# Half-Strassen first columns of the mixing product, and a new order of queue and products where attention ends and the branches begin

## The chip, the cores and the metric

The kernel runs on one core of a Trainium2 chip. The metric is the device time of one execution in microseconds (us). The five engines have one instruction stream each: PE (TensorE, matrix products), DVE (VectorE), ACT (ScalarE), POOL (GpSimd) and SP (SyncE, which here issues nearly all the DMA transfers). Each engine runs its own instructions in order, and they wait for each other through semaphores.

## The reference

The kernel computes one decoder block for 256 rows of width 2048 in float32. With the parts that the change leaves alone cut short:

```
proj = x @ w_in                         # 2048 columns each: bg, cg, hx, q, ..., ma, mb
y_a = (bg * causal_conv(cg * hx)) @ w_conv_out
y_b = sparse_attention(q, k, v, ...) @ w_attn_out
mixed = sigmoid(ma) * y_a + sigmoid(mb) * y_b
x = layer_norm(DN_ALPHA * x + mixed @ w_mix_out, ln1_g, ln1_b)
h = square(relu(x @ w_mlp_up)) @ w_mlp_down
ple = (p @ w_ple) * sigmoid(x @ w_ple_gate)
out = layer_norm(DN_ALPHA * x + h + ple, ln2_g, ln2_b)
```

## The kernel before

Every float32 operand of a matrix product is split into a high and a low part: ACT copies the high part, DVE subtracts it from the source to give the low part (`split`, L72 and L73). A product of two split operands takes three matmuls: high by high, low by high, high by low. The weights are read once from memory. `wchunk` (from L81) loads a chunk of 512 KB (`raw`, four buffers, DMA on SP, L85), copies it to `whi` (four buffers, ACT, L90) and subtracts to `wlo` (three buffers, DVE, L92). `xstat` takes 8 such chunks of 256 weight rows for 512 output columns: for each 128 weight rows it runs four matmuls with `whi` (L148, L149) and two with `wlo` (L152), and after the last chunk it evacuates two PSUM banks (one for each half of the 256 rows). `wstat` is the other layout (L110 with `whi`, L116 with `wlo`).

After attention come branch A (gate `ma`, weight `w_conv_out`, input `aT`) and branch B (gate `mb`, weight `w_attn_out`, input `oT`). In each branch, columns 0 to 1023 go as four blocks one after another: gate block 0 (L148 to L152 on `xT`, then a sigmoid on ACT, L707, into `sg`), out block 0 (L148 to L152 on `aT`, then a multiplication by `sg` on DVE, L776, into `ya`), gate block 1, out block 1. All four use PSUM banks 0 and 1, so the first matmul of a block waits for the evacuation of the block ahead of it. The gate's other 1024 columns are computed beside these blocks by Strassen's scheme (class `Seven`, L637 to L689, driven by `side()`): for each pair p of 128-row slices, a 1 MB load `rs` (L649, SP), sums of the input (`m` L714, `sa` L631 to L634), sums of the weights (`t`, L658 to L660), the splits of all of them into `forms` (L72, L73), and 18 matmuls (`products`, L676), where plain form takes 24. At the end `second` (L685) adds the seventh product, for which half of the weights are read again, and `close` combines the parts.

The two streams are interleaved by generators (`weave`, `next(sevens)`), but the order of the instructions on each engine is finally set by the compiler's scheduler, which simulates the kernel with its own costs; `after(ins)` tells it that an instruction may only come behind `ins` in that order.

After both branches the mixed rows (`mix`) are multiplied by `w_mix_out` in four plain `xstat` blocks of 512 columns (j = 0 to 3). Each is evacuated on DVE together with the residual `xres` (L861) and measured for the layer norm (L862).

Of the kernel before, what the change touches and what calls it, by code (L numbers as in the profile page):

```python
# [10 lines left out]
F32 = mybir.dt.float32  # L11
# [5 lines left out]
P = 128  # L17
# [28 lines left out]
def block_kernel(ctx: ExitStack, tc: tile.TileContext, x, p, w_in, conv_w, cmp_pe_k, cmp_w1_k, cmp_w2_k,  # L46
# [28 lines left out]

    last_hi, last_lo, last_whi, last_wlo, last_raw = [None], [None], [None], [None], [None]

# [3 lines left out]
    def wchunk(src, nk, n, behind=None):  # L81


        raw = wp.tile([P, nk, n], F32, tag="raw", name="raw", bufs=4)
        last_raw[0] = nc.sync.dma_start(raw, src).ins  # L85
        hi = wp.tile([P, nk, n], F32R, tag="whi", name="whi", bufs=4)
        lo = wp.tile([P, nk, n], F32R, tag="wlo", name="wlo", bufs=3)
        low, high = behind if isinstance(behind, tuple) else (behind, None)
        with after(high):
            last_whi[0] = nc.scalar.activation(hi, raw, AF.Copy).ins  # L90
        with after(low):
            last_wlo[0] = nc.vector.tensor_sub(lo, raw, f32(hi)).ins  # L92
        return hi, lo

    def wstat(src, c0, mov, evac, r0=0, nk=4, ahead=None, behind=None, ps=None):
# [6 lines left out]
        for k0 in range(0, KT, nk):  # L102
# [31 lines left out]

    def xstat(src, c0, n, sta, evac, r0=0, nkt=KT, ahead=None, behind=None, ps=None):

        if ps is None:
            ps = [mm([P, n]) for _ in range(NT)]
        for k2 in range(nkt // 2):
            hi, lo = wchunk(on_rows(src[r0 + k2 * 256:r0 + (k2 + 1) * 256, c0:c0 + n]), 2, n,  # L140
                            behind(k2) if behind is not None else None)
            for kk in range(2):
                kt = 2 * k2 + kk
                if ahead is not None:
                    ahead(kt)
                for t in range(NT):
                    ts = slice(t * P, (t + 1) * P)
                    nc.tensor.matmul(ps[t], sta[:, kt, 0, ts], hi[:, kk, :], start=(kt == 0), stop=False)  # L148
                    nc.tensor.matmul(ps[t], sta[:, kt, 1, ts], hi[:, kk, :], start=False, stop=False)  # L149
                for t in range(NT):  # L150
                    ts = slice(t * P, (t + 1) * P)
                    last_mm[0] = nc.tensor.matmul(ps[t], sta[:, kt, 0, ts], lo[:, kk, :], start=False,  # L152
                                                  stop=(kt == nkt - 1)).ins
            yield
        for t in range(NT):
            evac(t, ps[t])
# [44 lines left out]
    mhalf = const.tile([P, 1], F32, name="mhalf")  # L201
    nc.gpsimd.memset(mhalf, -0.5)

    X = big.tile([P, KT, 2, T], F32R, tag="X", name="xT")
# [268 lines left out]
    def attend(j, q):  # L473
# [111 lines left out]
        for g in range(4):  # L585
# [51 lines left out]
    class Seven:  # L637

        def __init__(self, rows, c0, mat, raw, t, forms, b, t0):
            self.rows, self.c0, self.mat, self.raw, self.t, self.forms, self.b, self.t0 = (
                rows, c0, mat, raw, t, forms, b, t0)
            self.raws, self.ts, self.sums, self.acc = {}, {}, {}, {}

        def load(self, p):
            self.raws[p] = self.raw(p)
            with after(last_raw[0]):
                nc.sync.dma_start(self.raws[p], self.rows[:, p, :, self.c0:self.c0 + 1024])  # L649

# [15 lines left out]
        def products(self, p, which):  # L666
            b, t0 = self.b(p), self.t0
            for n in which:
                first = (self.mat[:, 2 * p, :, 0:P] if n == 1 else self.mat[:, 2 * p + 1, :, P:] if n == 4 else
# [5 lines left out]
                for i, (a, w) in enumerate(((0, hi), (1, hi), (0, lo))):  # L675
                    last_mm[0] = nc.tensor.matmul(self.acc[n], first[:, a, :], self.forms[:, w, :],  # L676
                                                  start=(p == 0 and i == 0), stop=(p == 7 and i == 2)).ins

        def second(self, ps):

            for q in range(0, 8, 2):
                hi, lo = wchunk(self.rows[:, q:q + 2, 1, self.c0:self.c0 + 512], 2, 512)
                for k in range(2):
                    for i, (a, w) in enumerate(((0, hi), (1, hi), (0, lo))):
                        last_mm[0] = nc.tensor.matmul(ps, self.mat[:, 2 * (q + k) + 1, a, 0:P], w[:, k, :],  # L685
                                                      start=(q + k == 0 and i == 0),
                                                      stop=(q + k == 7 and i == 2)).ins
                yield
# [4 lines left out]
    def gate_seven(c_gate, raw):  # L693
        return Seven(in_pairs(w_in), c_gate + 1024, X, raw,
                     lambda p: [post.tile([P, 2, 512], F32, tag="m2", name="t") for _ in range(2)], None,
                     lambda p: 0, 4)

    def branch(c_gate, w, sta, sv, g, put, after_seven, last_two, close_at, meanwhile=lambda: iter(())):

        sg, forms = {}, sv.forms

        def gate_block(j):
            sg[j] = post.tile([P, NT, 512], F32, tag="sg", name="sg")
            return xstat(w_in, c_gate + j * 512, 512, X,
                         lambda t, ps: nc.scalar.activation(sg[j][:, t, :], ps, AF.Sigmoid), ps=[bank(0), bank(1)])  # L707
# [4 lines left out]
        def x_sums(p):  # L712
            m = post.tile([P, 2, T], F32, tag="pT", name="m", bufs=1)
            nc.vector.tensor_add(m, f32(X[:, 2 * p:2 * p + 2, 0, :]), f32(X[:, 2 * p:2 * p + 2, 1, :]))  # L714
            sv.sums[p] = forms[:, 12 + p % 2 * 2:14 + p % 2 * 2].rearrange("p a (c b t) -> p (a c) b t", c=2, b=2)
            sums_to(m, sv.sums[p])

        def side():

            if not sv.raws:  # L720
                sv.load(0)
                yield
            for i in range(4 * 8 + 1):
                p, r = divmod(i, 4)
                if r == 0 and p > 0:
                    sv.products(p - 1, (5, 7, 6, 4))
                if p < 8:
                    if r == 0:
                        x_sums(p)
                        sv.b_forms(p)  # L730
                    elif r == 1:
                        sv.t_sums(p)
                        if p < 7:
                            sv.load(p + 1)
                    elif r == 2:
                        sv.t_forms(p)
                    else:
                        sv.products(p, (1, 3))
                yield

        sevens = side()
# [99 lines left out]
    split(tp, pT[:, :, 0, :], pT[:, :, 1, :])  # L841
    C = post.tile([P, 2, NT * D], F32, tag="C", name="ple_gb", bufs=1)
    ple = C[:, 0].rearrange("p (t d) -> p t d", t=NT)
    gb = C[:, 1].rearrange("p (t d) -> p t d", t=2)
    y = post.tile([P, NT, D], F32, tag="Y", name="y", bufs=1)
# [10 lines left out]

    for j in range(4):
# [273 lines left out]
```

## Time and profile before

| | |
|---|---|
| Median of 3 runs | 1809.9 us (1809.32 to 1810.31) |
| Profiled execution, its own time | 1808.84 us |
| Span of its trace, first to last instruction | 1806.6 us |
| Busy share of PE, DVE, ACT | 99%, 74%, 55% |

The trace of one execution lies behind all the rows below. A matmul's own duration of 0.39 us is its latency through the array; a stream of matmuls of 512 columns starts one every 0.23 us, so it is the distance between starts that counts. In a timeline row, the text in square brackets is the idle time ahead of the instruction and what ended it. Rows named PEld, the weight loads, run beside the matmuls.

### The profile page before, as it was taken

The page shows a single profiled execution, that of the slowest core. Times are in us where ns is not written, and L with a number is a line of the kernel's source. Part 1 is how long each engine was busy: PE and PEld are TensorE (multiplying, and loading weights), DVE is VectorE, ACT ScalarE, POOL GpSimd, SP SyncE. Part 2 cuts the span into 40 slices and gives each one's busy share as a digit, 9 for nine tenths or more (in the row PEclk, how much of TensorE's full clock was granted, in tenths as well). Part 3 has the DMA queues.
Part 4 walks back from the last instruction along what each step waited for, and adds up shares of the span by engine and source line. Part 5 has one row for each costly group of instructions (what it writes and reads, how often), then busy time and mean ns, then how long its engine had stood idle before and what let it go on. Part 6 is the DMA issues. An engine that isn't in the chain of part 4 may idle for free.

```text
span 1806.6 us, 24945 instructions
## 1 busy us (share of the span) xinstructions
PE 1790.7 (99%) x9292; PEld 1534.9 (85%) x9292; DVE 1339.0 (74%) x1964; ACT 989.8 (55%) x1342; POOL 18.4 (1%) x33
## 2 busy tenths in 40 slices
PE   9999999999999999999999999999999999999997
PEld 7889888888888788888888888888888888888886
DVE  6776776767787996897755668886898689865564
ACT  5555555555555555555443745764676467646640
POOL 1000000000000000000000000000000000000000
PEclk9999999999999999999999999999999999999999
DMA  8777665566655665866655577754865586567671
GB/s 258 225 239 210 183 176 164 164 182 179 175 163 173 200 233 176 278 201 225 193 183 195 176 242 239 228 187 162 281 209 163 186 268 216 173 205 219 220 242 54
DMA packets 256121, 363.41 MB, mean 201 GB/s; under 512 B 10837, under 2 KB 175541, under 8 KB 255232
## 3 DMA queue, kind: packets, MB, share of 16 engines
q1 hardware_dynamic: 250944, 348.30, 61.5%
q0 software_dynamic: 2112, 8.81, 1.4%
q10 hardware_dynamic: 2944, 4.72, 0.8%
q8 instruction: 73, 1.20, 0.3%
q14 instruction: 48, 0.39, 0.1%
HBM read 359.66 MB, written 2.12 MB: 200 GB/s over the span
## 4 chain that ended last, share of the span: by engine, by line
PE 99%; DVE 0%; ACT 0%; DMA 0%; issue 0%; SPq 0%; DVEq 0%
PE mm L110 16%; PE u L110 9%; PE s L676 9%; PE mm L116 8%; PE u L148 7%; PE u L149 7%; PE u L152 7%; PE u L116 5%; PE s L152 5%; PE s L149 5%; PE s L148 5%; PE s L110 4%; PE s L116 2%; PE s L685 2%; PE s L1073 1%; PE pss L497 1%
## 5 line engine op out<-in xcount | busy, mean ns | idle before, releaser
L92 DVE TENSOR_TENSOR wlo<-raw,whi 128x1024 fp32r<-128x1024 f32 (+2 forms) x588 | 702.0, 1201 | 305.6 <-issue 69.0
L90 ACT ACTIVATE whi<-raw 128x1024 fp32r<-128x1024 f32 (+2 forms) x588 | 612.1, 1043 | 530.2 <-PE u L149 160.8
L110 PE MATMUL mm<-xT,whi 128*128 128x512 f32 x1280 | 313.2, 393 | 0.0
L110 PEld LDWEIGHTS mm<-xT,whi 128*128 128x128 f32 x1280 | 234.0, 189 | 44.7 <-ACT whi L90 0.6
L110 PE MATMUL u<-x,whi 128*128 128x512 f32 x736 | 190.7, 391 | 0.0
L116 PE MATMUL mm<-xT,wlo 128*128 128x256 f32 x1280 | 181.6, 285 | 0.6 <-DVE wlo L92 0.6
L116 PEld LDWEIGHTS mm<-xT,wlo 128*128 128x128 f32 x1280 | 169.8, 190 | 8.2 <-DVE wlo L92 0.8
L110 PEld LDWEIGHTS u<-x,whi 128*128 128x128 f32 x736 | 132.5, 188 | 23.2
L116 PEld LDWEIGHTS u<-x,wlo 128*128 128x128 f32 x736 | 101.8, 190 | 8.2
L116 PE MATMUL u<-x,wlo 128*128 128x256 f32 x736 | 104.2, 282 | 0.0
L73 DVE TENSOR_TENSOR forms<-tr,forms 128x1024 fp32r<-128x1024 f32 x68 | 81.7, 1221 | 16.1 <-ACT forms L72 15.8
L72 ACT ACTIVATE forms<-tr 128x1024 fp32r<-128x1024 f32 x68 | 70.4, 1050 | 18.3 <-PE s L676 8.6
L676 PE MATMUL s<-forms,sums 128*128 128x512 f32 x288 | 73.0, 390 | 0.0
L110 PE MATMUL s<-x,whi 128*128 128x512 f32 x288 | 71.6, 392 | 0.0
L676 PEld LDWEIGHTS s<-forms,sums 128*128 128x128 f32 x288 | 53.7, 188 | 11.1
L148 PE MATMUL s<-whi,h 128*128 128x512 f32 x160 | 62.2, 389 | 0.0
L149 PE MATMUL s<-whi,h 128*128 128x512 f32 x160 | 62.2, 389 | 0.0
L110 PEld LDWEIGHTS s<-x,whi 128*128 128x128 f32 x288 | 52.2, 188 | 9.7
L148 PE MATMUL u<-whi,xT 128*128 128x512 f32 x128 | 49.9, 390 | 0.6 <-DVE cg L463 0.6
L149 PE MATMUL u<-whi,h 128*128 128x512 f32 x128 | 49.8, 389 | 0.0
L149 PE MATMUL u<-whi,xT 128*128 128x512 f32 x128 | 49.8, 389 | 0.0
L676 PE MATMUL s<-forms 128*128 128x512 f32 x192 | 49.6, 389 | 0.0
(347 smaller groups left out, 2990.4 us busy)
## 6 DMA issues: line engine op xcount, KB each, us to landing
raw<-in_w_in_dram SPq DMA_DIRECT2D x204, 512.0 KB, 4.4
raw<-in_w_mlp_up_dram SPq DMA_DIRECT2D x128, 512.0 KB, 4.6
raw<-in_w_mlp_down_dram SPq DMA_DIRECT2D x84, 512.0 KB, 4.1
raw<-in_w_conv_out_dram SPq DMA_DIRECT2D x32, 512.0 KB, 4.3
raw<-in_w_attn_out_dram SPq DMA_DIRECT2D x32, 512.0 KB, 4.4
raw<-in_w_mix_out_dram SPq DMA_DIRECT2D x32, 512.0 KB, 3.7
raw<-in_w_ple_gate_dram SPq DMA_DIRECT2D x32, 512.0 KB, 4.4
rs<-in_w_mlp_down_dram SPq DMA_DIRECT2D x12, 1024.0 KB, 7.3
```

What stands on the lines that cost most here:

```text
L72: last_hi[0] = nc.scalar.activation(hi, src, AF.Copy).ins
L73: last_lo[0] = nc.vector.tensor_sub(lo, src, f32(hi)).ins
L90: last_whi[0] = nc.scalar.activation(hi, raw, AF.Copy).ins
L92: last_wlo[0] = nc.vector.tensor_sub(lo, raw, f32(hi)).ins
L110: last_mm[0] = nc.tensor.matmul(ps[f].rearrange("p a t -> p (a t)"), hi[:, kk, f * P:(f + 1) * P], mov[:, k0 + kk].rearrange("p a t -> p ( ...
L116: last_mm[0] = nc.tensor.matmul(ps[f][:, 1, :], lo[:, kk, f * P:(f + 1) * P], mov[:, k0 + kk, 0, :], start=False, stop=False, skip_group_c ...
L148: nc.tensor.matmul(ps[t], sta[:, kt, 0, ts], hi[:, kk, :], start=(kt == 0), stop=False)
L149: nc.tensor.matmul(ps[t], sta[:, kt, 1, ts], hi[:, kk, :], start=False, stop=False)
L152: last_mm[0] = nc.tensor.matmul(ps[t], sta[:, kt, 0, ts], lo[:, kk, :], start=False, stop=(kt == nkt - 1)).ins
L497: nc.tensor.matmul(ps, q[:, g, a, t * P:(t + 1) * P], kT[:, j, c, c0:c0 + n], start=(i == 0), stop=(i == 2))
L676: last_mm[0] = nc.tensor.matmul(self.acc[n], first[:, a, :], self.forms[:, w, :], start=(p == 0 and i == 0), stop=(p == 7 and i == 2)).ins
L685: last_mm[0] = nc.tensor.matmul(ps, self.mat[:, 2 * (q + k) + 1, a, 0:P], w[:, k, :], start=(q + k == 0 and i == 0), stop=(q + k == 7 and ...
```

## The change

- `Seven` takes a number of pairs n, and a new object `sv_mix` with n = 4 computes rows 0 to 1023 of columns 0 to 1023 of the mixing product by Strassen's scheme, beside the plain blocks for columns 1024 to 2047. Rows 1024 to 2047 of the first columns stay plain (`mix_block` with k0 = 8). `mix_close` combines the parts. Its 1 MB loads are named `tr`. `side` moves out of `branch`.
- The residual `xres` moves to another place in memory (tag C), behind `oT`.
- Where attention ends: the first gate chunk is issued by `prefetch` inside the last attention turn; the first `rs`, `m`, `sa`, `sg` and `t` get the first places of the new pool; a sigmoid of one column (`mhalf1`) stands ahead of the branches; and the fifth chunk of gate block 0 may be issued only behind the first `rs` load (`held`).
- `seven_a.lag = 1`: in branch A the products come one step later in the order, and each may only stand behind the last matmul that was written before it (`behind`).
- `wstat`: the last chunk of a projection with `ahead` (the first one only) takes the high part ahead of the low part.

```
         raw = wp.tile([P, nk, n], F32, tag="raw", name="raw", bufs=4)
-        last_raw[0] = nc.sync.dma_start(raw, src).ins
+        with after(held[0]):
+            last_raw[0] = nc.sync.dma_start(raw, src).ins
+        held[0] = None
...
             last = k0 + nk == KT
-            parts_ = (low, high) if last or ahead is None and k0 // nk % 2 == 1 else (high, low)
+            parts_ = (low, high) if last and ahead is None or ahead is None and k0 // nk % 2 == 1 else (high, low)
...
+    def prefetch():
+        first_piece.append(wchunk(on_rows(w_in[:256, C_MA:C_MA + 512]), 2, 512))
+        yield
+    first_piece = []
...
-            weave(chain(*dense), evenly(20, 4 * len(dense)), attend(j, q))
+            weave(chain(*dense), evenly(20, 4 * len(dense)) + [23] * (j == 3),
+                  chain(attend(j, q), prefetch()) if j == 3 else attend(j, q))
...
+    rs0 = post.tile([P, 2, 1024], F32, tag="rs", name="rs", bufs=1)
+    m0 = post.tile([P, 2, T], F32, tag="pT", name="m", bufs=1)
+    sa0 = post.tile([P, 4, P], F32, tag="pn", name="sa", bufs=1)
     ya = post.tile([P, NT, D], F32, tag="Y", name="ya", bufs=1)
+    sg0 = [post.tile([P, NT, 512], F32, tag="sg", name="sg") for _ in range(2)]
+    t0 = [post.tile([P, 2, 512], F32, tag="m2", name="t") for _ in range(2)]
+    with after(last_hi[0]):
+        nc.scalar.activation(mhalf1, mhalf, AF.Sigmoid)
...
         def products(self, p, which):
             b, t0 = self.b(p), self.t0
+            behind = last_mm[0] if self.lag else None
             for n in which:
                 first = (self.mat[:, 2 * p, :, 0:P] if n == 1 else self.mat[:, 2 * p + 1, :, P:] if n == 4 else
                          self.sums[p][:, {5: 0, 6: 1, 7: 2, 3: 3}[n]])
...
                 if p == 0:
                     self.acc[n] = bank({1: 2, 3: 3, 5: 4, 7: 5, 6: 6, 4: 7}[n])
                 for i, (a, w) in enumerate(((0, hi), (1, hi), (0, lo))):
-                    last_mm[0] = nc.tensor.matmul(self.acc[n], first[:, a, :], self.forms[:, w, :],
-                                                  start=(p == 0 and i == 0), stop=(p == 7 and i == 2)).ins
+                    with after(behind):
+                        last_mm[0] = nc.tensor.matmul(self.acc[n], first[:, a, :], self.forms[:, w, :],
+                                                      start=(p == 0 and i == 0), stop=(p == self.n - 1 and i == 2)).ins
...
+    def side(sv, tag):
...
+        for _ in range(sv.lag):
+            yield
+        for i in range(4 * sv.n + 1):
+            p, r = divmod(i, 4)
...
+        ahead_of = None
+        if not sv.raws:
+            sv.load(0)
+            ahead_of, first_load = 3, sv.last_load
+        sevens = side(sv, "pT")
         for j in range(2):
             for block in (lambda: gate_block(j), lambda: out_block(j, [bank(0), bank(1)])):
-                for _ in block():
+                for i, _ in enumerate(block()):
                     next(sevens)
+                    if i == ahead_of:
+                        held[0], ahead_of = first_load, None
...
-    seven_a = gate_seven(C_MA, lambda p: post.tile([P, 2, 1024], F32, tag="rs", name="rs", bufs=1))
+    seven_a = gate_seven(C_MA, lambda p: post.tile([P, 2, 1024], F32, tag="rs", name="rs", bufs=1) if p else rs0)
+    seven_a.lag = 1
...
-    xres = big.tile([P, NT, D], F32, tag="O", name="xres")
+    xres = post.tile([P, NT, D], F32, tag="C", name="xres", bufs=1)
...
+    sv_mix = Seven(in_pairs(w_mix_out), 0, mix, lambda p: tr[-1][:, p % 2],
+                   lambda p: [post.tile([P, 2, 512], F32, tag="m2", name="t") for _ in range(2)],
+                   big.tile([P, 16, 512], F32R, tag="X", name="forms"), lambda p: 0, 4, n=4)
+    def mix_block(j, banks, k0=0, ahead=None):
         cs = slice(j * 512, (j + 1) * 512)
-        def ev_mix(t, ps):
-            nc.vector.scalar_tensor_tensor(y[:, t, cs], xres[:, t, cs], ALPHA, ps, op0=ALU.mult, op1=ALU.add)
+        def ev(t, ps):
+            if k0:
+                nc.vector.tensor_add(y[:, t, cs], y[:, t, cs], ps)
+            else:
+                nc.vector.scalar_tensor_tensor(y[:, t, cs], xres[:, t, cs], ALPHA, ps, op0=ALU.mult, op1=ALU.add)
             nc.vector.bn_stats(stats[:, t, j, :], y[:, t, cs])
-        run(xstat(w_mix_out, j * 512, 512, mix, ev_mix, ahead=mix_turn({4: (3, sg[3], 0), 8: (3, sg[3], 2)}) if j == 0 else None))
+        return xstat(w_mix_out, j * 512, 512, mix, ev, r0=k0 * P, nkt=KT - k0, ps=banks, ahead=ahead, kt0=k0)
+    def mix_close():
+        a = sv_mix.acc
+        u = [post.tile([P, 2, 512], F32, tag="m2", name="u") for _ in range(2)]
+        u2, u3, u4 = u[0][:, 0], u[0][:, 1], u[1][:, 0]
+        at = [(t, slice(c, c + 512)) for t in range(2) for c in (0, 512)]
+        y00, y01, y10, y11 = (y[:, t, c] for t, c in at)
+        x00, x01, x10, x11 = (xres[:, t, c] for t, c in at)
+        nc.scalar.activation(u2, a[1], AF.Copy)
+        for dst, v, w, op in ((y00, x00, a[1], ALU.add), (u2, u2, a[6], ALU.add), (u4, u2, a[5], ALU.add),
+                              (y11, x11, a[5], ALU.add), (y01, x01, a[3], ALU.add), (u3, u2, a[7], ALU.add),
+                              (y10, x10, a[4], ALU.subtract), (y01, y01, u4, ALU.add), (y10, y10, u3, ALU.add),
+                              (y11, y11, u3, ALU.add)):
+            with after(last_wlo[0]):
+                if v in (x00, x01, x10, x11):
+                    nc.vector.scalar_tensor_tensor(dst, v, ALPHA, w, op0=ALU.mult, op1=op)
+                else:
+                    nc.vector.tensor_tensor(dst, v, w, op=op)
+        yield
+        ps = bank(4)
+        for i, _ in enumerate(sv_mix.second(ps)):
+            if i < 1:
+                yield
+        nc.vector.tensor_add(y00, y00, ps)
+        yield
+    sv_mix.load(0)
+    weave(chain(mix_block(2, [bank(0), bank(1)], ahead=mix_turn({4: (3, sg[3], 0), 8: (3, sg[3], 2)})),
+                mix_block(3, [bank(0), bank(1)]), mix_block(0, [bank(0), bank(1)], 8),
+                mix_block(1, [bank(2), bank(3)], 8)),
+          list(range(20)), chain(side(sv_mix, "sg"), mix_close()))
+    C = post.tile([P, 2, NT * D], F32, tag="C", name="ple_gb", bufs=1)
+    ple = C[:, 0].rearrange("p (t d) -> p t d", t=NT)
+    gb = C[:, 1].rearrange("p (t d) -> p t d", t=2)
```

How the instructions stand on the engines before and after is shown at two places. Names: `raw`, `whi` and `wlo` are a weight chunk and its parts, `rs` the load for the products, `m` and `sa` sums of the input, `t` sums of the weights, `forms` their split parts. Line numbers of the changed kernel differ: L86 is L85 of before, L94 is L92, L672 is L649, L681 to L683 are L658 to L660, L727 is L714, L654 to L657 are L631 to L634, L153, L154 and L157 are L148, L149 and L152, L701 is L676, L760 is L707.

First place: the end of attention and gate block 0. On SP, the queue of loads, before:

```order
L85 DMA raw<-in_w_in_dram 128x2x512 x8
L649 DMA rs<-in_w_in_dram 128x2x1024
L85 DMA raw<-in_w_conv_out_dram 128x2x512 x4
L649 DMA rs<-in_w_in_dram 128x2x1024
L85 DMA raw<-in_w_conv_out_dram 128x2x512 x3
```

The same place on SP now:

```order
L86 DMA raw<-in_w_in_dram 128x2x512 x4
L672 DMA rs<-in_w_in_dram 128x2x1024
L86 DMA raw<-in_w_in_dram 128x2x512 x4
L672 DMA rs<-in_w_in_dram 128x2x1024
L86 DMA raw<-in_w_conv_out_dram 128x2x512 x4
```

The first `rs` load has moved ahead of chunks 5 to 8 of gate block 0.

On DVE at the same place, from the first `m` of branch A, before (the first `wlo` here is that of chunk 5):

```order
L714 TENSOR_TENSOR m<-xT 128x512
L92 TENSOR_TENSOR wlo<-raw,whi 128x1024
L631 TENSOR_TENSOR sa<-m 128x128
L633 TENSOR_TENSOR sa<-m 128x128
L632 TENSOR_TENSOR sa<-sa,m 128x128
L634 TENSOR_TENSOR sa<-m,sa 128x128
L714 TENSOR_TENSOR m<-xT 128x512
L92 TENSOR_TENSOR wlo<-raw,whi 128x1024
L658 TENSOR_TENSOR t<-rs 128x1024
```

On DVE now, from the sixth instruction behind that first `m` on (the `wlo` at the end is that of chunk 5):

```order
L73 TENSOR_TENSOR forms<-sa,forms 128x4x128
L654 TENSOR_TENSOR sa<-m 128x128
L656 TENSOR_TENSOR sa<-m 128x128
L655 TENSOR_TENSOR sa<-sa,m 128x128
L681 TENSOR_TENSOR t<-rs 128x1024
L657 TENSOR_TENSOR sa<-m,sa 128x128
L73 TENSOR_TENSOR forms<-rs,forms 128x1024
L682 TENSOR_TENSOR t<-rs,t 128x512
L727 TENSOR_TENSOR m<-xT 128x512
L73 TENSOR_TENSOR forms<-t,forms 128x1024
L683 TENSOR_TENSOR t<-t,rs 128x512
L94 TENSOR_TENSOR wlo<-raw,whi 128x1024
```

The `wlo` of chunk 5, which stood ahead of the first instruction that needs `rs`, now stands behind seven instructions that begin with it.

Second place: the end of gate block 0 and the start of out block 0 in branch A. On PE, before (`u<-wlo,xT` is gate block 0, `u<-whi,aT` is out block 0, `s<-forms` are the products):

```order
L149 MATMUL u<-whi,xT 128x512
L152 MATMUL u<-wlo,xT 128x512 x2
L676 MATMUL s<-forms 128x512
L676 MATMUL s<-forms,xT 128x512 x3
L676 MATMUL s<-forms 128x512 x2
L676 MATMUL s<-forms,xT 128x512
L676 MATMUL s<-forms 128x512 x5
L148 MATMUL u<-whi,aT 128x512
```

On PE now:

```order
L153 MATMUL u<-whi,xT 128x512
L154 MATMUL u<-whi,xT 128x512
L153 MATMUL u<-whi,xT 128x512
L154 MATMUL u<-whi,xT 128x512
L157 MATMUL u<-wlo,xT 128x512 x2
L153 MATMUL u<-whi,aT 128x512
```

The twelve products that stood between the two blocks have moved into the blocks; nothing stands between the last matmul of the one and the first of the other.

On ACT at this place, now (`sg<-u` is the evacuation of gate block 0):

```order
L72 ACTIVATE forms<-t 128x1024
L72 ACTIVATE forms<-sa 128x4x128
L92 ACTIVATE whi<-raw 128x1024 x2
L760 ACTIVATE sg<-u 128x512 x2
L92 ACTIVATE whi<-raw 128x1024
```

Two chunk copies (L92) stand directly ahead of the two sigmoids; before, a split (`forms<-t`) and the table load of the sigmoid stood there.

## Rows read from the trace of the kernel before

**Rows 1.** The page: busy times, and engines of the chain that ended last.

```profile
PE 1790.7 (99%) x9292; PEld 1534.9 (85%) x9292; DVE 1339.0 (74%) x1964; ACT 989.8 (55%) x1342; POOL 18.4 (1%) x33
...
PE 99%; DVE 0%; ACT 0%; DMA 0%; issue 0%; SPq 0%; DVEq 0%
```

**Rows 2.** Waits of PE: us in total, times, longest us.

```profile
PE u L148 <- ACT sg L707: 0.7, 1, 0.7
PE mm L116 <- DVE wlo L92: 0.6, 1, 0.6
```

**Rows 3.** Windows: length, busy PE, PEld, DVE, ACT, POOL, granted clock, DMA share, GB/s.

```profile
625.00:650.00 25.00, 25.00 (x112) 20.70 (x111) 25.00 (x34) 14.67 (x16) 0.00 (x0) 1.00 0.64 213
915.00:940.00 25.00, 25.00 (x118) 20.69 (x117) 14.55 (x17) 10.68 (x12) 0.00 (x0) 1.00 0.54 177
940.00:1005.00 65.00, 65.00 (x289) 53.81 (x288) 36.01 (x37) 25.25 (x25) 0.00 (x0) 1.00 0.59 193
```

**Rows 4.** Timeline of the mixing product: start us, duration us, engine, line, instruction.

```profile
999.76 0.39 PE L148 MATMUL s<-whi,mix 128*128 128x512 f32 x1
...
1001.12 0.39 PE L148 MATMUL s<-whi,mix 128*128 128x512 f32 x1
```

**Rows 5.** Timeline of the first projection's last chunk.

```profile
21.53 0.68 DVE L92 TENSOR_TENSOR wlo<-raw,whi 128x512 fp32r<-128x512 f32 x1
22.27 0.74 PE L116 MATMUL mm<-xT,wlo 128*128 128x256 f32 x4 [0.63 <-DVE wlo L92]
22.84 0.40 PE L110 MATMUL mm<-xT,whi 128*128 128x512 f32 x1
```

**Rows 6.** Timeline of the end of attention and gate block 0.

```profile
578.28 0.87 PE L576 MATMUL po<-pT,vn 128*128 128x256 f32 x6
...
579.22 0.37 SPq L649 DMA_DIRECT2D rs<-in_w_in_dram  x1
...
584.45 1.22 DVE L658 TENSOR_TENSOR t<-rs 128x1024 f32<-128x1024 f32 x1 [0.64 <-DMA rs<-in_w_in_dram]
...
585.59 0.68 DVE L73 TENSOR_TENSOR forms<-sa,forms 128x512 fp32r<-128x512 f32 x1
585.80 0.62 PE L152 MATMUL u<-wlo,xT 128*128 128x512 f32 x2
...
586.19 1.22 DVE L73 TENSOR_TENSOR forms<-rs,forms 128x1024 fp32r<-128x1024 f32 x1
```

**Rows 7.** Timeline of the end of gate block 0 and the start of out block 0.

```profile
599.62 0.39 PE L676 MATMUL s<-forms,xT 128*128 128x512 f32 x1
600.04 1.04 ACT L90 ACTIVATE whi<-raw 128x1024 fp32r<-128x1024 f32 x1
...
600.99 1.04 ACT L72 ACTIVATE forms<-t 128x1024 fp32r<-128x1024 f32 x1
...
602.05 1.28 ACT L707 ACT_TABLE_LOAD   x1
...
603.34 1.09 ACT L707 ACTIVATE sg<-u 128x512 f32<-128x512 f32 x2
...
603.99 0.50 PE L148 MATMUL u<-whi,aT 128*128 128x512 f32 x1 [0.70 <-ACT sg L707]
```

**Rows 8.** DVE's instructions by line and form, 570 to 915 us: busy us, mean ns, idle before.

```profile
L92 DVE TENSOR_TENSOR wlo<-raw,whi 128x1024 fp32r<-128x1024 f32 x104 | 126.8, 1221 | 40.3 <-PE u L152 21.3 <-PE s L152 10.2 <-issue 4.6
...
L714 DVE TENSOR_TENSOR m<-xT 128x512 f32<-128x512 f32 x16 | 11.0, 684 | 3.4 <-PE po L576 3.4
...
L631 DVE TENSOR_TENSOR sa<-m 128x128 f32<-128x128 f32 x16 | 4.5, 284 | 0.0
...
L776 DVE TENSOR_TENSOR ya<-u,sg 128x512 f32<-128x512 f32 x4 | 2.6, 685 | 1.3 <-PE u L152 1.3
```

**Rows 9.** PE's timeline at the start of the kernel.

```profile
6.84 2.05 PE L110 MATMUL mm<-xT,whi 128*128 128x512 f32 x4
8.68 1.06 PE L116 MATMUL mm<-xT,wlo 128*128 128x256 f32 x4
```

More of the change, by code (lines that the diff above doesn't have):

```diff
@@ L74, in split @@
         return last_lo[0]
-    last_hi, last_lo, last_whi, last_wlo, last_raw = [None], [None], [None], [None], [None]
+    last_hi, last_lo, last_whi, last_wlo, last_raw, held = ([None] for _ in range(6))
     def on_rows(src):
@@ L133, in wstat, with xstat @@
             evac(f, ps[f][:, 0, :], ps[f][:, 1, :])
-    def xstat(src, c0, n, sta, evac, r0=0, nkt=KT, ahead=None, behind=None, ps=None):
+    def xstat(src, c0, n, sta, evac, r0=0, nkt=KT, ahead=None, behind=None, ps=None, kt0=0, first=None):
         if ps is None:
@@ L139, in xstat @@
         for k2 in range(nkt // 2):
-            hi, lo = wchunk(on_rows(src[r0 + k2 * 256:r0 + (k2 + 1) * 256, c0:c0 + n]), 2, n,
-                            behind(k2) if behind is not None else None)
+            if first is not None and k2 == 0:
+                hi, lo = first
+            else:
+                hi, lo = wchunk(on_rows(src[r0 + k2 * 256:r0 + (k2 + 1) * 256, c0:c0 + n]), 2, n,
+                                behind(k2) if behind is not None else None)
             for kk in range(2):
@@ L147, in xstat @@
                     ts = slice(t * P, (t + 1) * P)
-                    nc.tensor.matmul(ps[t], sta[:, kt, 0, ts], hi[:, kk, :], start=(kt == 0), stop=False)
-                    nc.tensor.matmul(ps[t], sta[:, kt, 1, ts], hi[:, kk, :], start=False, stop=False)
+                    nc.tensor.matmul(ps[t], sta[:, kt0 + kt, 0, ts], hi[:, kk, :], start=(kt == 0), stop=False)
+                    nc.tensor.matmul(ps[t], sta[:, kt0 + kt, 1, ts], hi[:, kk, :], start=False, stop=False)
                 for t in range(NT):
                     ts = slice(t * P, (t + 1) * P)
-                    last_mm[0] = nc.tensor.matmul(ps[t], sta[:, kt, 0, ts], lo[:, kk, :], start=False,
+                    last_mm[0] = nc.tensor.matmul(ps[t], sta[:, kt0 + kt, 0, ts], lo[:, kk, :], start=False,
                                                   stop=(kt == nkt - 1)).ins
@@ L202, in block_kernel @@
     nc.gpsimd.memset(mhalf, -0.5)
+    mhalf1 = const.tile([P, 1], F32, name="mhalf1")
     X = big.tile([P, KT, 2, T], F32R, tag="X", name="xT")
@@ L637, in block_kernel, with __init__ @@
     class Seven:
[L641 to L644, printed above, removed]
+        def __init__(self, rows, c0, mat, raw, t, forms, b, t0, n=8):
+            self.rows, self.c0, self.mat, self.raw, self.t, self.forms, self.b, self.t0, self.n = (
+                rows, c0, mat, raw, t, forms, b, t0, n)
+            self.raws, self.ts, self.sums, self.acc, self.lag = {}, {}, {}, {}, 0
         def load(self, p):
@@ L648, in load @@
             with after(last_raw[0]):
-                nc.sync.dma_start(self.raws[p], self.rows[:, p, :, self.c0:self.c0 + 1024])
+                self.last_load = nc.sync.dma_start(self.raws[p], self.rows[:, p, :, self.c0:self.c0 + 1024]).ins
         def b_forms(self, p):
@@ L686, in second @@
                                                       start=(q + k == 0 and i == 0),
-                                                      stop=(q + k == 7 and i == 2)).ins
+                                                      stop=(q + k == self.n - 1 and i == 2)).ins
                 yield
@@ L696, in gate_seven, with x_sums @@
                      lambda p: 0, 4)
+    def side(sv, tag):
+        def x_sums(p):
+            m = post.tile([P, 2, T], F32, tag=tag, name="m", bufs=1 if tag == "pT" else 2)
+            nc.vector.tensor_add(m, f32(sv.mat[:, 2 * p:2 * p + 2, 0, :]), f32(sv.mat[:, 2 * p:2 * p + 2, 1, :]))
+            sv.sums[p] = sv.forms[:, 12 + p % 2 * 2:14 + p % 2 * 2].rearrange("p a (c b t) -> p (a c) b t", c=2, b=2)
+            sums_to(m, sv.sums[p])
+        for _ in range(sv.lag):
+            yield
+        for i in range(4 * sv.n + 1):
+            p, r = divmod(i, 4)
+            if r == 0 and p > 0:
+                sv.products(p - 1, (5, 7, 6, 4))
+            if p < sv.n:
+                if r == 0:
+                    x_sums(p)
+                    sv.b_forms(p)
+                elif r == 1:
+                    sv.t_sums(p)
+                    if p < sv.n - 1:
+                        sv.load(p + 1)
+                elif r == 2:
+                    sv.t_forms(p)
+                else:
+                    sv.products(p, (1, 3))
+            yield
     def branch(c_gate, w, sta, sv, g, put, after_seven, last_two, close_at, meanwhile=lambda: iter(())):
-        sg, forms = {}, sv.forms
+        sg = {}
         def gate_block(j):
@@ L706, in gate_block @@
             return xstat(w_in, c_gate + j * 512, 512, X,
-                         lambda t, ps: nc.scalar.activation(sg[j][:, t, :], ps, AF.Sigmoid), ps=[bank(0), bank(1)])
+                         lambda t, ps: nc.scalar.activation(sg[j][:, t, :], ps, AF.Sigmoid), ps=[bank(0), bank(1)],
+                         first=first_piece.pop() if first_piece else None)
         def out_block(j, banks, ahead=None):
             return xstat(w, j * 512, 512, sta, lambda t, ps: put(j, t, ps, sg[j][:, t, :]), ps=banks, ahead=ahead)
[L712 to L741, printed above, removed]
+        ahead_of = None
[3 more added lines that the diff above has]
+        sevens = side(sv, "pT")
         for j in range(2):
             for block in (lambda: gate_block(j), lambda: out_block(j, [bank(0), bank(1)])):
-                for _ in block():
+                for i, _ in enumerate(block()):
                     next(sevens)
+                    if i == ahead_of:
+                        held[0], ahead_of = first_load, None
         run(sevens)
@@ new lines, in mix_close @@
+    def mix_close():
[13 more added lines that the diff above has]
+                    nc.vector.scalar_tensor_tensor(dst, v, ALPHA, w, op0=ALU.mult, op1=op)
+                else:
+                    nc.vector.tensor_tensor(dst, v, w, op=op)
[5 more added lines that the diff above has]
+        nc.vector.tensor_add(y00, y00, ps)
+        yield
```

7 lines of the change are left out of this document (2 added, 5 removed).

## The prediction

> **What bounds the kernel now.** I read the page first, then PE's waits, then timelines of the places that the change touches, and last windows for the density of DVE. The page says that PE is busy for 99% of the span and that the chain that ended last is 99% PE [rows 1]. So a microsecond is won only by fewer matmuls or by a wait of PE that goes, and lost by a wait of PE that comes. The waits are few and short: in the stretch that is changed, one of 0.7 us for a sigmoid and one of 0.6 us for a `wlo` [rows 2]. The price of a matmul is the distance of starts: from 999.76 to 1001.12 us six of them begin, L148 to L152 and two more, so 1.36 / 6 = 0.227 us [rows 4]. DVE, which prepares the products, has 50.6 of 90 us busy in the mixing product but 25.00 of 25 in a stretch of branch A, and PE still does not wait there [rows 3].
>
> **Mixing product.** Before: 4 blocks x 16 slices x 6 = 384 matmuls. Now: 192 for the last two column blocks, 96 for the plain half of the first two, 4 pairs x 18 = 72 products and 12 for the seventh, together 372. Twelve fewer at 0.227 are -2.7 us. On DVE each pair costs `m` 0.68, four `sa` at 0.28, the split of the sums 0.68, of the weights 1.22, `t` 1.22 + 0.68 + 0.68 and two splits at 1.22, together 8.7 us (128x1024 forms at 1.22, 128x512 at 0.68, 128x128 at 0.28) [rows 8]. Four pairs are 34.9, the close adds 11 operations at 0.68 or 7.5, and six `wlo` fewer (eight chunks go, two come for the seventh product) take off 7.3. The 50.6 us become 85.7, in about 87 us. That is close to full. As the branch ran at 25.00 of 25 without a wait [rows 3], and as the preparation of the first pairs stands in branch B's last block, I take 0. Bounds: 0, and for blocks 2 and 3 alone (half of the old 50.6 + 34.9 = 60.2, with the two turns of `mix` some 2.7 more, against 264 matmuls or 59.9) 3 us, 5 with the 2 that the last closing operations could add behind the last matmul. `xres` is loaded later, by ACT, 2 MB that are needed only at the first evacuation some 27 us (120 matmuls) on; I count nothing, and price a miss as part of the 5.
>
> **First projection.** PE waits to 22.27 for a `wlo` that DVE starts at 21.53 and ends at 22.21, and then does four low matmuls [rows 5]. With the four high ones first (4 x 0.227 = 0.9 us) this time is filled, and the wait of 0.6 us goes: -0.6 (bounds -0.8 and 0). Late next is the same `wlo`, which is then done ahead of its reader by 0.3 us.
>
> **The old waits around 600 us.** Between 599.62 and 603.99 us PE starts 11 matmuls, 2.49 us of work in 4.37 us, so 1.88 us go to waits, for `forms` and for the sigmoid behind a table load of 1.28 us [rows 7]. The table load moves ahead of the branch (the one-column sigmoid `mhalf1`), where ACT has time, and the products stand one step later, so their forms are there: -1.9 (bounds -1.9 and -1.2, with the `forms` waits kept).
>
> **Start of branch A: a new wait.** In the order of SP the first `rs` load stands ahead of chunks 5 to 8. It still waits for the last matmul of attention, L576: before, it was issued at 579.22, right behind that matmul's end at 579.15, and landed at 584.45 [rows 6]. Its new place in the pool does not free it, since the semaphore that its row in the order waits for still counts to that matmul. So `rs` does not come earlier, and what is queued behind it comes later. On DVE the `wlo` of chunk 5 stands behind the seven instructions that begin with `t<-rs`. In one stream such instructions start 1.14 us apart for 128x1024 (584.45 to 585.59) and 0.60 for 128x512 (585.59 to 586.19) [rows 6]; `sa` I take at 0.2. From the landing: 1.14 + 0.2 + 1.14 + 0.6 + 0.6 + 1.14 + 0.6 = 5.4, so the `wlo` begins at 589.9 and ends at 591.1. PE wants it at 585.80 [rows 6], and its order has nothing else there: 591.1 - 585.8 = +5.3 us. Behind the waiting L152 stand the rest of gate block 0 and the products; behind the `wlo` on DVE the next two, which PE then reaches later than they end. ACT is less late: the chunk's raw data, half as large, lands by estimate half of 5.2 us behind `rs`, the `whi` copy of 1.04 us is done near 588.2 [rows 6, 7], and four matmuls of chunk 5 fall into the wait. Bounds: 0, if the order on DVE costs nothing, and 6.9, an estimate, if `rs` takes 30% longer than its 5.2 us beside the loads that are now issued right behind it. [...]
>
> **Block ends in branch A: three new waits.** All blocks share banks 0 and 1. Before, products stood between the blocks and filled PE's time while ACT or DVE emptied the banks. Now they stand in closed groups inside the blocks, and PE goes straight from the last L152 to the next L148. The least that this costs is latency 0.39, sigmoid 0.59 (half of 1.09 [rows 7] and a little) and 0.1 for two hand-overs, less the two starts of L152 in between, 0.45: 0.6 us, and 0.7 with the multiplication of 0.68 [rows 8], so 2.0 us for three ends (gate to out, out to gate, gate to out). But the order on ACT has a chunk copy of 1.04 us [rows 7] directly ahead of the sigmoid, and that copy waits for a `whi` buffer, which the last L149 of the block frees. From that L149's start: 0.39 + 0.08, copy 0.95 (600.04 to 600.99 [rows 7]), sigmoid 0.65 (603.34 to 603.99) make 2.07, where 0.68 is free of a wait: 1.4 us. At the out block's end a `t` of 0.60 and a `sa` stand ahead of the multiplication on DVE: 1.4 likewise. Sum 1.4 + 1.4 + 1.4 = +4.2; bounds 2.0 and 4.5.
>
> **Sum.** -2.7 - 0.6 - 1.9 + 5.3 + 4.2 = +4.3. The profiled execution took 1808.8 us, so 1813.1 for one like it. The median lies 1.1 above that execution, so 1814.2 against 1809.9.
>
> **Rivals.**
> 1. No wait at the start of branch A. The reason for it: `rs` and `m` have places of their own now, and an early load would have DVE past its seven instructions in time. The wait is away if `rs` lands 5.3 us earlier, at 579.1, so if it is issued by 573.9, before L576 [rows 6]. Against it stands that its row waits for PE. The sum is then -5.2 + 2.0 to 4.2, some 1807 to 1809 on the median; with the block ends covered too, 1804.7. This is the side of not slower.
> 2. The block ends cost only their least, 2.0, if the copies ahead of the sigmoid are done before the last matmul. The order speaks against it. Sum +2.1, 1812.
> 3. DVE becomes the bound in the mixing product: with 85.7 of 87 us it decides as soon as the operations there stand 3% worse than now. It adds 3 to 5 us to the forecast: 1817 to 1819.
> 4. PE falls to half speed after the long wait. At the start of the kernel four matmuls take 1.84 us (6.84 to 8.68) [rows 9], 0.46 for one where the mixing product has 0.227 [rows 4], so such a stretch costs 0.23 us for each matmul. In the new wait PE runs four matmuls in 6 us; twenty slow ones behind it would add 4 to 5: 1818 to 1819. Against it: the windows keep a granted clock of 1.00, the full 2.4 GHz [rows 3]; but the longest of PE's waits in the rows is 0.7 us [rows 2]. The Trainium skill ("TensorE: Matmul & The Clock Gate", Part 1: The HAM clock gate) says that an idle array falls to 1.2 GHz and comes back after sustained work; no run here shows it in mid-kernel.
>
> **Chances.** About 0.2% (3.6 us) is what a measurement of this kernel can tell from no change: faster is below 1806.3, slower above 1813.5. The forecast with its own range of 1811.5 to 1817 has 0.50, of which 0.35 slower and 0.15 within. Rival 1 has 0.16: 0.09 faster, 0.07 within. Rival 2 has 0.14, all within. Rival 3 has 0.12 and rival 4 has 0.08, all slower. Together faster 0.09, within 0.36, slower 0.55. The range leaves out the lower half of rival 1 and the upper edge of rivals 3 and 4: 1808.5 to 1819.
>
> **What would show it.** In the trace after, PE's waits should have one of 5 us for `wlo` near 585 us, three of 0.6 to 1.5 us at the block ends of branch A, for the sigmoid twice and once for `ya`, and no row for the `wlo` at 22 us. The mixing product should show no wait of PE over 0.5 us and DVE near full. The prediction is wrong if `rs` is issued before the last matmul of attention, or if DVE has PE wait in the mixing product.

## The result and the profile after

The changed kernel takes 1821.5 us in the median of 5 runs (1817.8 to 1822.7), against 1809.9. The ratio to before is 1.0059, with a 95% interval of 1.0048 to 1.0071: slower, by 11.6 us between the medians (by the interval, 8.7 to 12.9). Forecast were +4.3 us and a range that ended at 1819. The direction was right, the size was not. The profiled execution of the changed kernel took 1822.32 us, 13.5 more than that of before; it is one of the longer of its executions, so the trace shows them and not the two of 1818.

The waits of PE tell most of it. Columns: who waited for what; us in total, times, longest us. These rows answer to [rows 2]:

```profile
PE s L701 <- ACT forms L72: 3.1, 1, 3.1
PE u L153 <- ACT whi L92: 2.4, 1, 2.4
PE u L153 <- ACT sg L760: 2.4, 2, 1.2
PE u L157 <- DVE wlo L94: 2.2, 1, 2.2
PE u L153 <- DVE ya L808: 1.6, 1, 1.6
```

The `wlo` row of the first projection is gone. Four of these five rows stand where waits were forecast: `whi` and `wlo` at the start of branch A, `sg` twice (before, one wait of 0.7) and `ya` once at the block ends. The first row, 3.1 us for `forms`, was not forecast; it lies in the mixing product. The windows show where it is idle, and one thing more, the granted clock (the number behind POOL's):

```profile
570.00:620.00 50.00, 43.59 (x184) 34.88 (x183) 40.03 (x60) 27.00 (x34) 0.00 (x0) 0.93 0.59 202
620.00:700.00 80.00, 77.26 (x340) 63.37 (x339) 66.04 (x83) 40.84 (x42) 0.00 (x0) 1.00 0.61 196
...
915.00:1020.00 105.00, 101.94 (x451) 83.97 (x450) 86.91 (x113) 50.15 (x54) 0.00 (x0) 0.98 0.61 211
```

Two of the three stretches have a granted clock below 1.00. PE's own timeline at the start of branch A shows why (start us, duration, instruction, idle before):

```profile
583.91 0.61 PE L157 MATMUL u<-wlo,xT 128*128 128x512 f32 x2
586.95 0.50 PE L153 MATMUL u<-whi,xT 128*128 128x512 f32 x1 [2.42 <-ACT whi L92]
...
590.32 1.22 PE L157 MATMUL u<-wlo,xT 128*128 128x512 f32 x2 [2.16 <-DVE wlo L94]
591.35 0.63 PE L153 MATMUL u<-whi,xT 128*128 128x512 f32 x1
591.77 0.63 PE L154 MATMUL u<-whi,xT 128*128 128x512 f32 x1
592.20 0.63 PE L153 MATMUL u<-whi,xT 128*128 128x512 f32 x1
```

PE does four matmuls in the 5.8 us from 584.5 to 590.3. Then matmuls start 0.43 us apart (591.35 to 591.77 to 592.20) where [rows 4] have 0.227, and the granted clock of this stretch is 0.50, the lower of the two clock levels, 1.2 GHz:

```profile
590.00:594.00 4.00, 3.68 (x9) 2.90 (x10) 4.00 (x5) 1.21 (x2) 0.00 (x0) 0.50 0.92 304
```

The 14 matmuls from 590.32 to 595.96 took 5.64 us instead of 3.2, so the slow clock cost about 2.4 us.

The mixing product, on PE (the second row here is the wait of 3.1 us), has the same two steps, a wait and slow matmuls behind it:

```profile
936.93 0.38 PE L226 MATMUL s<-ident,g 128*128 128x128 f32 x2
940.37 1.22 PE L701 MATMUL s<-forms 128*128 128x512 f32 x2 [3.06 <-ACT forms L72]
...
942.25 0.63 PE L153 MATMUL u<-whi,mix 128*128 128x512 f32 x1
942.67 0.63 PE L154 MATMUL u<-whi,mix 128*128 128x512 f32 x1
```

Who was late? Rows of SP, ACT and DVE in the same stretch:

```profile
928.77 0.46 SPq L672 DMA_DIRECT2D tr<-in_w_mix_out_dram  x1
...
928.88 0.39 ACTq L869 DMA_DIRECT2D xres<-in_x_dram  x1
...
931.03 1.06 ACT L92 ACTIVATE whi<-raw 128x1024 fp32r<-128x1024 f32 x1 [1.11 <-DMA raw<-in_w_mix_out_dram]
...
938.75 1.06 ACT L92 ACTIVATE whi<-raw 128x1024 fp32r<-128x1024 f32 x1 [6.66 <-DMA raw<-in_w_mix_out_dram]
939.71 0.61 ACT L72 ACTIVATE forms<-sa 128x512 fp32r<-128x512 f32 x1
940.35 0.69 DVE L73 TENSOR_TENSOR forms<-sa,forms 128x512 fp32r<-128x512 f32 x1 [1.88 <-ACT forms L72]
```

ACT stood still for 6.66 us for a weight chunk. The split that the products need (939.71) stands behind that chunk's copy in ACT's order, though it does not need the chunk. That chunk was issued at 928.35 and took 10.3 us to land. At 928.77 and 928.88 a 1 MB load and the 2 MB residual were issued, beside it. Before, the residual was issued at 849 us, 90 us ahead of its first use at 939. The transfers of 915 to 960 us (KB each, median us to landing):

```profile
raw<-in_w_mix_out_dram SPq DMA_DIRECT2D x12, 512.0 KB, 5.3
tr<-in_w_mix_out_dram SPq DMA_DIRECT2D x2, 1024.0 KB, 10.4
xres<-in_x_dram ACTq DMA_DIRECT2D x1, 2048.0 KB, 12.8
```

Last, a block end in branch A (gate block 0 to out block 0), which answers to [rows 7]:

```profile
606.39 0.61 PE L157 MATMUL u<-wlo,xT 128*128 128x512 f32 x2
606.63 1.06 ACT L92 ACTIVATE whi<-raw 128x1024 fp32r<-128x1024 f32 x1 [1.70 <-PE u L154]
...
607.60 1.07 ACT L760 ACTIVATE sg<-u 128x512 f32<-128x512 f32 x2
...
608.23 0.50 PE L153 MATMUL u<-whi,aT 128*128 128x512 f32 x1 [1.23 <-ACT sg L760]
```

The copy waits for the last L154, the sigmoid waits for the copy, PE waits for the sigmoid. Without a wait PE would start at 606.84, so 1.39 us go, where the prediction had 1.4.

### The profile page after: what moved, and what is told of

It is laid out like the page before. It is cut to its first block, busy times and chain, and to the rows that moved or that the text cites. A ratio compares the mean times of both kernels' runs of the same rounds, so it can differ in the third digit from the quotient of the medians.

```text
span 1820.4 us, 24994 instructions
## 1 busy us (share of the span) xinstructions
PE 1793.6 (99%) x9280; PEld 1535.2 (84%) x9280; DVE 1368.6 (75%) x2017; ACT 998.2 (55%) x1354; POOL 18.4 (1%) x33
## 4 chain that ended last, share of the span: by engine, by line
PE 60%; DMA 1%; DVE 1%; issue 0%; ACT 0%; DVEq 0%; SPq 0%; ACTq 0%
PE s L701 9%; PE u L112 9%; PE u L153 6%; PE u L157 6%; PE u L154 6%; PE u L118 5%; PE s L157 4%; PE s L153 4%; PE s L154 4%; PE s L112 3%; PE s L118 2%; PE s L710 2%; PE s L1145 1%; DMA raw<-in_w_mix_out_dram 1%; DMA raw<-in_w_mlp_up_dram 0%; PE s L226 0%
## 5 line engine op out<-in xcount | busy, mean ns | idle before, releaser
L94 DVE TENSOR_TENSOR wlo<-raw,whi 128x1024 fp32r<-128x1024 f32 (+2 forms) x582 | 693.8, 1200 | 279.7 <-issue 65.9
L92 ACT ACTIVATE whi<-raw 128x1024 fp32r<-128x1024 f32 (+2 forms) x582 | 605.2, 1043 | 527.3 <-PE u L154 159.8
L73 DVE TENSOR_TENSOR forms<-tr,forms 128x1024 fp32r<-128x1024 f32 x72 | 86.5, 1219 | 15.9 <-ACT forms L72 15.9
L72 ACT ACTIVATE forms<-tr 128x1024 fp32r<-128x1024 f32 x72 | 74.6, 1051 | 23.7 <-PE s L701 10.1
L701 PE MATMUL s<-forms,sums 128*128 128x512 f32 x288 | 73.1, 390 | 0.3 <-ACT sums L72 0.3
L701 PE MATMUL s<-forms 128*128 128x512 f32 x240 | 61.1, 392 | 3.1 <-ACT forms L72 3.1
L701 PEld LDWEIGHTS s<-forms,sums 128*128 128x128 f32 x288 | 53.7, 188 | 11.6 <-ACT sums L72 0.5
L154 PE MATMUL s<-whi,h 128*128 128x512 f32 x160 | 62.2, 389 | 0.0
L153 PE MATMUL s<-whi,h 128*128 128x512 f32 x160 | 62.2, 389 | 0.0
L701 PEld LDWEIGHTS s<-forms 128*128 128x128 f32 x240 | 45.4, 190 | 12.7 <-ACT forms L72 3.3
L153 PE MATMUL u<-whi,xT 128*128 128x512 f32 x128 | 50.6, 395 | 4.6 <-ACT whi L92 2.4
L73 DVE TENSOR_TENSOR forms<-t,forms 128x1024 fp32r<-128x1024 f32 x40 | 48.7, 1220 | 7.1 <-ACT forms L72 6.1
```

What stands on the lines that cost most here:

```text
L72: last_hi[0] = nc.scalar.activation(hi, src, AF.Copy).ins
L73: last_lo[0] = nc.vector.tensor_sub(lo, src, f32(hi)).ins
L153: nc.tensor.matmul(ps[t], sta[:, kt0 + kt, 0, ts], hi[:, kk, :], start=(kt == 0), stop=False)
L154: nc.tensor.matmul(ps[t], sta[:, kt0 + kt, 1, ts], hi[:, kk, :], start=False, stop=False)
```

## The experiments

**Without rs ahead of the chunks.** Theory 1 is the order of loads, theory 2 the new places and the rule on products.

```
-                        held[0], ahead_of = first_load, None
+                        ahead_of = None
```

> The changed kernel without the rule that the fifth chunk of gate block 0 may only come behind the first rs load; chunks 5 to 8 stand ahead of rs again. Theory 1 (rs ahead of the chunks and its preparation ahead of chunk 5's low part make the wait at the start of branch A, and the half clock of about 13 matmuls behind it follows from that wait): PE's waits of 2.4 us for whi and 2.2 us for wlo near 585 us go, the granted clock of 570 to 620 us is 1.00 instead of 0.93, and 5 + 2.4 = 7 us come off: about 1814. Theory 2 (the new places and the product rule alone make that wait): it stays, about 1821.

Measured: 1815.7 us (ratio to before 1.0039, 1.0026 to 1.0051), 5.8 less than the changed kernel, where the first theory had 7. The waits near 585 us are gone, so the order of the loads, with what follows it on DVE, makes them. But the block ends became worse, which neither theory had:

```profile
PE u L153 <- ACT sg L760: 3.6, 2, 2.4
PE s L701 <- ACT forms L72: 2.7, 1, 2.7
PE u L153 <- DVE ya L808: 2.1, 1, 2.1
```

At the first block end ACT now waits until 597.52 for `rs`, and the splits of `rs` and `t` and a chunk copy stand ahead of the sigmoid:

```profile
597.52 1.06 ACT L72 ACTIVATE forms<-rs 128x1024 fp32r<-128x1024 f32 x1 [2.79 <-DMA rs<-in_w_in_dram]
...
600.38 1.06 ACT L760 ACTIVATE sg<-u 128x512 f32<-128x512 f32 x2
```

In its windows the clock is 1.00 from 590 to 620 us, with the wait of 2.4 us in it, and 1.00 from 925 to 945 with the one of 2.7. But behind the wait of 2.1 us, which ends at 633.34, it falls:

```profile
620.00:635.00 15.00, 12.89 (x55) 10.33 (x54) 15.00 (x21) 7.25 (x8) 0.00 (x0) 0.96 0.81 288
635.00:645.00 10.00, 10.00 (x41) 8.15 (x40) 7.07 (x10) 4.50 (x5) 0.00 (x0) 0.90 0.51 128
```

A wait of this length is followed by slow matmuls at times, and at times not, and it is not always the longer wait that has them.

**The residual loaded later, in two halves.** Two 1 MB loads on SP's queue, the first one chunk behind the third `tr`, the second eight loads later. (The scheduler also moved a part of PE's order there.)

```
-    nc.scalar.dma_start(xres, x.rearrange("(t p) d -> p t d", p=P))
+    def x_load(c, at, turn=lambda kt: None):
+        def ahead(kt):
+            turn(kt)
+            if kt == at:
+                with after(last_raw[0]):
+                    nc.sync.dma_start(xres[:, :, c:c + 1024], ...)
+        return ahead
-    weave(chain(mix_block(2, ..., ahead=mix_turn(...)), mix_block(3, ...), ...
+    weave(chain(mix_block(2, ..., ahead=x_load(1024, 12, turn3)), mix_block(3, ..., ahead=x_load(0, 10)), ...
```

> The changed kernel with the 2 MB residual load cut in two 1 MB loads that stand on SP's queue, the first behind the chunks of the first mixing block, the second half a block later. Theory 1 (the 2 MB load that ACT issues at 928.9 us, beside a 1 MB load and the chunks, delays a chunk from 4 to 10 us and so makes the 3.3 us wait in the mixing product and the slow matmuls behind it): the wait at 937 us shrinks below 1 us and 4 us come off: about 1817.5. Theory 2 (DVE is full in the mixing product and makes the wait): it stays, about 1821.5.

Measured: 1816.6 us (1.0039, 1.0024 to 1.0054), 4.9 less, where the first theory had 4. The mixing product has no wait, PE is busy for all of it and the clock is 1.00, with DVE busier than in the changed kernel (91.6 of 105 us against 86.9):

```profile
915.00:1020.00 105.00, 105.00 (x472) 86.91 (x471) 91.61 (x121) 53.84 (x59) 1.41 (x1) 1.00 0.62 212
```

Theory 1 holds, as far as the residual goes. DVE was not the bound. The split still stands behind a chunk's copy in ACT's order, but the copy waits 2.04 us for its chunk instead of 6.66:

```profile
933.24 1.06 ACT L92 ACTIVATE whi<-raw 128x1024 fp32r<-128x1024 f32 x1 [2.04 <-DMA raw<-in_w_mix_out_dram]
934.20 0.62 ACT L72 ACTIVATE forms<-sa 128x512 fp32r<-128x512 f32 x1
```

The landing times of the chunks of 915 to 960 us, of the changed kernel and of this run, have the same median and another longest:

```profile
DMA to landing us min/median/max: 3.5/5.3/10.3
DMA to landing us min/median/max: 4.0/5.3/6.9
```

Time, queue and size of the residual load changed together here; which of them counts was not tested.

**The mixing product alone.** The kernel before with the Strassen half of the mixing product and the moved residual; lag, rule, `held`, `prefetch`, the first places, the early sigmoid and the order of `parts_` are all taken back.

> The kernel before with the half-Strassen mixing product and the moved residual alone, none of the changes at the start. Theory 1 (the loss has two places that do not depend on each other): start and block ends as before, twelve matmuls fewer, the wait of 3.3 us and slow matmuls in the mixing product: 1809.9 - 2.7 + 5 + 1 = about 1813. Theory 2 (the mixing product waits only because the stages ahead of it are disturbed): no wait there, about 1807.5.

Measured: 1810.6 us, and 1.0005 with an interval of 0.9996 to 1.0015: no difference from before that can be told. The time lies midway between the two forecasts, 1813 and 1807.5, and decides nothing; the trace does. It has the wait in the mixing product on its own, and so theory 2 is out:

```profile
PE s L692 <- ACT forms L72: 2.8, 1, 2.8
PE u L153 <- ACT sg L751: 1.7, 1, 1.7
```

The twelve matmuls saved are paid back there. The loss of 12 us against before comes from the other parts.

**Without the lag and its rule.**

```
-    seven_a.lag = 1
+    seven_a.lag = 0
```

> The changed kernel without the lag of one step and without the rule that binds each product of branch A behind the matmul written before it. Theory 1 (that rule empties the block ends): products stand between the blocks again, the three waits of 1.3 to 1.7 us at 607, 638 and 670 us fall to under 0.5 each: about 1818. Theory 2 (the block ends wait for ACT and DVE whatever stands between): about 1821.5.

Measured: 1809.5 us (1.0000, 0.9991 to 1.0010), 12 less than the changed kernel, more than three times the 3.5 that I expected. The block ends are filled, as theory 1 said, and PE is busy for all of 590 to 700 us:

```profile
620.00:700.00 80.00, 80.00 (x355) 66.26 (x354) 69.32 (x91) 43.54 (x48) 0.00 (x0) 1.00 0.60 199
```

But the wait at the start of branch A shrank too, though `rs` still stands ahead of the chunks:

```profile
583.00 0.61 PE L157 MATMUL u<-wlo,xT 128*128 128x512 f32 x2
583.87 0.73 PE L701 MATMUL s<-forms,xT 128*128 128x512 f32 x2 [0.25 <-ACT forms L72]
584.44 1.87 PE L701 MATMUL s<-forms 128*128 128x512 f32 x6
586.15 0.39 PE L701 MATMUL s<-forms,xT 128*128 128x512 f32 x1
...
589.45 0.73 PE L157 MATMUL u<-wlo,xT 128*128 128x512 f32 x2 [1.00 <-DVE wlo L94]
590.02 0.40 PE L153 MATMUL u<-whi,xT 128*128 128x512 f32 x1
```

Twelve products of the first pair fill the time in which chunk 5 is late; 1 us of wait is left for `wlo`, and the clock does not fall (590.02 follows at full rate). Between the two traces (1822.3 and 1811.4 us) lie 11.0 us. The start cost 5.05 and 2.4 for the clock, of which 1.25 are left, and the block ends 4.45, together 10.7. The wait in the mixing product stays, with 3.4 us.

**The lag without the rule.**

```
-            behind = last_mm[0] if self.lag else None
+            behind = None
```

> The changed kernel with the lag of one step kept, but without the rule that binds a product of branch A behind the matmul written before it. Theory 1 (the binding rule alone empties PE's order at the start of branch A and at the block ends): as the run without lag and rule, about 1809.5, with 2 to 3 us of wait near 585 us and none at the block ends. Theory 2 (the lag of one step does it): about 1821.

Measured: 1810.0 us (1.0003, 0.9994 to 1.0012). The rule does it, not the step alone; the rule without the step was not run.

**Both causes out, and the place of rs.** Three kernels without the lag and with the later residual: `rs` after four chunks of gate block 0 (as in the changed kernel), after all eight (as before), and after six (`ahead_of, first_load = 5, sv.last_load`).

> The changed kernel without lag and binding rule, and with the residual load cut in two and moved behind chunks on SP's queue. Theory 1 (the two losses add up, and each has its own cause): 1809.5 - 4.8 = about 1804.7, faster than before, with no wait over 0.5 us in the mixing product. Theory 2 (with one wait gone the next one in the mixing product takes its place): about 1808 to 1809.

> As the run before, and chunks 5 to 8 ahead of the first rs load again. Theory 1 (with products free to move, the place of rs matters for about 2 us of wait at the start of branch A, and costs up to 2 us at the first block end instead): 1804 to 1806, within 1.5 us of the run before. Theory 2 (rs ahead of the chunks is a loss in any case): 2.5 us faster than the run before, about 1802.

> As the run without lag and with the later residual load, but rs stands behind the sixth chunk instead of the fourth. If the wait at the start of branch A comes from the low part of chunk 5 standing behind the preparation of rs, it goes, and the early rs still keeps the products ready at the first block end: about 1803. If only the landing of rs counts, it is as the run with rs behind all eight chunks, 1804 to 1806.

| rs stands | median us | ratio to before, interval |
|---|---|---|
| after four chunks | 1807.3 | 0.9987, 0.9979 to 0.9996 |
| after eight chunks | 1805.2 | 0.9975, 0.9965 to 0.9985 |
| after six chunks | 1804.8 | 0.9976, 0.9965 to 0.9986 |

The two causes add up only in part. With `rs` after four chunks the first theory had 1804.7 and the second 1808 to 1809; the median of 1807.3 lies between them, 2.2 under the kernel without lag, where the same move had given 4.9 on the changed kernel. Between the traces it is 4.9 (1806.5 against 1811.4), and PE's wait in the mixing product is gone; but the trace without lag is that of one of its longest executions (1807.1 to 1811.4). What the wait costs in the short ones is not known, since no trace shows one. `rs` ahead of chunk 5 is a loss of 2.1 us even with free products, and the wait for `sg` at the first block end, which the first theory set against it, is only 0.2 us behind eight chunks; the second theory, with 2.5, came nearer, though its time of 1802 was not reached. Between six and eight no difference can be told. In the last run the wait at the start of branch A is gone, as its first theory had it, but the time lies in the 1804 to 1806 of its second. The last two kernels beat both, by 3.9 and 4.3 us against the 1809.1 that the kernel before took beside them. The last one's waits of PE, all that are left in the whole kernel:

```profile
PE pw L290 <- DVE tab L304: 1.5, 1, 1.5
PE tp L226 <- DMA xnat<-in_x_dram: 1.1, 2, 0.6
PE u L153 <- DVE cg L469: 0.6, 1, 0.6
PE mm L153 <- ACT whi L92: 0.3, 1, 0.3
PE s L701 <- DVE forms L73: 0.2, 1, 0.2
```

All five have a row of about the same size before the change. What is gained fits the forecast's own savings, 5.2 us in all: twelve matmuls (2.7), the wait of the first projection and most of the old waits around 600 us. They were not measured one by one.

## Why the prediction was wrong

- **Start of branch A, +5.3.** Right in place, cause and size: behind 583.91 PE had six matmuls to go to the L157 of chunk 5, so 585.27 (0.227 each), and got it at 590.32, 5.05 later. "its order has nothing else there" was the point on which it rested, and the run without the lag and its rule shows its weight: with products there, two waits of 0.25 and 1.0 us are left. What came on top was rival 4, the half clock, with 2.4 us of its 4 to 5; I had given it 0.08. It had twenty slow matmuls where about twelve came, at 0.20 us each instead of 0.23. The Trainium skill ("TensorE: Matmul & The Clock Gate", Part 1: The HAM clock gate) says that the clock of an idle array falls to 1.2 GHz; the trace agrees, with matmuls 0.43 us apart behind the wait and a granted clock of 0.50 there.
- **Block ends, +4.2.** Right. From the rows at 606, 638 and 669 us the distances are 1.39, 1.72 and 1.34 above the free ones, together 4.45. The middle one was longer: DVE, busy without a gap, came to `ya` only at 639.18, behind a `wlo`, a `t` and a `sa`.
- **Mixing product, 0.** This is the step that failed: "`xres` is loaded later, by ACT, 2 MB that are needed only at the first evacuation some 27 us (120 matmuls) on; I count nothing". The load was in time for its own reader. It was another transfer that it made late: beside it and a 1 MB load, a chunk took 10.3 us from issue to landing instead of some 4, ACT waited 6.66 us for it, and the split behind it in ACT's order came 3 us late for PE. With 3.06 us of wait and some 1.75 of slow matmuls behind it the stretch cost about 4.8 us in this trace; moving the load gave 4.9 of the median back. The prediction's own sign, no wait of PE over 0.5 us in the mixing product, failed here, though not through DVE, which it named. The price stood in the bounds as "part of the 5", under rival 3, whose mechanism, a full DVE, the same run rules out. The range took rivals 3 and 4 one at a time; the half clock and a price like rival 3's came together, and that is more than the 1819 at which it ended.
- **First projection, -0.6, and the old waits, -1.9.** The `wlo` row is gone, and so are the waits for `forms` and the table load; what stands at 607 us now is the block end.
- **Sum.** -2.7 - 0.6 - 1.9 + 5 + 4.45 come to 4.3, as forecast. With 2.4 for the clock and 4.8 in the mixing product they make 11.5 of the 13.5 us between the two traces. The rest is not settled: it lies in stretches the change does not touch, among them 0.7 us where the layer norm ends and 0.6 at a later load, which were not tested.

The half clock is shown as a consequence of the waits (it goes wherever they go), but not what decides whether a wait of 2 to 3 us brings it. The spread of the runs does not settle it either: the kernels with the wait in the mixing product differ by 4 to 5 us from run to run (1807.1 to 1811.4 in the run without lag) and the four without it and with the moved residual by 0.8 to 2.4 us, but the kernel before, which has no such wait, differs by 4.8 us in 27 runs (1808.2 to 1813.0).

## What to carry to other kernels

A load that is in time for its own reader still has a price where the queue is dense: ask which other transfer lands later, which engine stands still for it in order, and what is queued behind that. A rule that binds work to fixed places can take away the filler with which an engine bridges a wait; test it together with every wait that the change may add. And a wait of PE of several microseconds costs more than its length, for the matmuls behind it can run at half rate.

## What was not expected of the hardware

A 2 MB load with a 1 MB load beside 512 KB chunks stretched a chunk's transfer from about 4 to 10.3 us, and the 1 MB load's to 13.4 (issue to landing, 928.35 and 928.77 us); with the residual in halves and later, in the run of that name, no chunk takes over 7, and that 1 MB load takes 8.1. The clock fell to half after a wait of 5 us with four matmuls in it, after one of 3.1 us, after one of 2.8 (the mixing product alone, 0.91 from 925 to 945 us) and after one of 2.1 (`rs` not ahead), but not after those of 2.4 and 2.7 in that last run.
